# Moving the weights and the staging buffers of a matmul with batch normalisation to multiples of 512 bytes in each partition

## The chip, the cores and the metric

The kernel runs on one core of one Trainium2 chip. The metric is the time of one execution on the device, in microseconds (us); several executions are timed and their median is given. The span that a profile quotes is some 2 us shorter than the timed value, for it runs from the first to the last recorded instruction.

## The reference

The product of x and the weights is normalised per column over all 8192 rows.

```python
batch, m, k, n = 16, 512, 1024, 768          # x: (16, 512, 1024), weight: (1024, 768), float32
y = np.matmul(x, weight)
mean = np.mean(y, axis=(0, 1), keepdims=True)
var = np.var(y, axis=(0, 1), keepdims=True)
y_norm = (y - mean) / np.sqrt(var + eps)
return (gamma * y_norm + beta).astype(np.float32)
```

## The kernel before

The 768 columns are six tiles of 128, and the columns stand on the partitions, so the statistics of a column are sums along one partition. x comes in as bf16 (the DMA casts) through four **staging** buffers of 6144 bytes per partition. VectorE turns it, two bf16 at a time as one float32, into xT, in which even and odd elements of the contraction therefore alternate. TensorE multiplies w (stationary, 128 columns a time) with every second element of xT. When a tile's statistics are complete, y is scaled, transposed back by TensorE, copied as float32 into the *same* staging buffers and stored. The first three column tiles are stored together, in pieces of 384 float32 (1536 B) per row; the last three one at a time, in pieces of 128 float32 (512 B).

```python
    singles = ctx.enter_context(tc.tile_pool(name="singles", bufs=1))
    stage = ctx.enter_context(tc.tile_pool(name="stage", bufs=STAGE))      # STAGE = 4
    xtpool = ctx.enter_context(tc.tile_pool(name="xtpool", bufs=C - EARLY))
    ypool = ctx.enter_context(tc.tile_pool(name="ypool", bufs=...))
    # ... cut
    ident = singles.tile([P, P], bf16)
    eps_sb = singles.tile([P, 1], f32)
    idle_sb = singles.tile([P, CH], bf16)              # operand of the warm-up matmuls
    w_sb = singles.tile([P, JW, 2, N], bf16)
    stats = singles.tile([P, NT, C, 6], f32)
    # ... cut: nine small tiles

    def load_x(q):
        x_bf = stage.tile([P, QT, KQ], bf16, tag="st")
        # ... cut: four DMAs from GpSimd, 32 partitions each

    def mm(nt, c):
        # ... cut
                seq(nc.tensor.matmul(
                    y_ps, w_sb[:, jw, e, nt * P:(nt + 1) * P], xT[c][:, jw, :, e],
                    start=(jw == 0 and e == 0), stop=(jw == JW - 1 and e == 1),
                ))

    def out_copy(key, part, parts, eng):
        # ... cut
            o_sb = stage.tile([P, parts] + list(src.shape[1:]), f32, tag="st")
        # ... cut: ScalarE or VectorE copies the transposed tile from PSUM into o_sb
    def store(key, nts, m0, tiles):
        # ... cut: one DMA of the sync engine from o_sb to the output
```

Tiles are laid out in each partition in the order in which pools and tiles are made. So w came to stand at byte 17824, which is 416 past a multiple of 512, and the staging buffers at 32736, 38880, 45024 and 51168, all 480 past one.

## Time and profile before

| | before |
|---|---|
| time, median of 4 | 230.71 us (230.02 to 231.17) |
| span of the profile | 228.4 us |
| TensorE busy | 207.4 us, 91% |
| last piece of w lands, long run of matmuls starts | 19.56, 19.70 us |
| last matmul of the chain starts | 205.83 us |
| from there to the end of the span | 22.57 us |

The chain that ended last is read in order of time: each line is a start, a length and what held the end up then. Its lines and the DMA rates are shown in the prediction. One line more of the chain of before is of use below, the first transpose back, after the long unbroken run of whole-width matmuls:

```profile
128.65 0.43 PE o_ps L211 x6
```

So the middle has two parts: matmuls alone, 19.70 to 128.65 us, and matmuls mixed with transposes, 128.65 to 205.83 us.

### The profile page before, as it was taken

To read this page: it belongs to the slowest core of one execution; us is meant where nothing else is said; L and a number is where in the kernel's file an instruction comes from. 1 tells how busy PE (TensorE), PEld (TensorE's weight loads), DVE (VectorE), ACT (ScalarE), POOL (GpSimd) and SP (SyncE) were. 2 spreads that over 40 slices of the span, in tenths; PEclk is the share of its full clock that TensorE was granted. 3 is DMA by queue.
4 is the path that set the end of the run, shared out by engine and by line. 5 is a ranking of instruction groups with operands and counts; after the bars stand their busy time and mean duration, and the time that the engine had idled before them with its cause. 6 is when DMAs were issued, how large, how long until landed. Compare 5 with 4: busy or idle time off the path is not lost.

```text
span 228.4 us, 3323 instructions
## 1 busy us (share of the span) xinstructions
PE 207.4 (91%) x1238; PEld 106.0 (46%) x1238; DVE 142.1 (62%) x252; ACT 100.7 (44%) x155; POOL 88.5 (39%) x160
## 2 busy tenths in 40 slices
PE   7767999999999999999999999999999999994720
PEld 2432685444444444444444565655555545553610
DVE  0223769677675777677845968686754476537940
ACT  2001424134233233332633599987696736674310
POOL 8887787678687786878500000000000000003000
PEclk9999999999999999999999999999999999999555
DMA  5999999999999999999000079999989933887996
GB/s 58 180 191 175 191 170 185 173 170 167 161 186 179 167 184 186 163 188 158 1 0 0 4 264 366 362 366 366 337 257 281 258 92 86 225 243 196 270 282 176
DMA packets 69345, 43.75 MB, mean 192 GB/s; under 512 B 3280, under 2 KB 68816, under 8 KB 69328
## 3 DMA queue, kind: packets, MB, share of 16 engines
q0 software_dynamic: 35904, 18.37, 61.3%
q1 hardware_dynamic: 33424, 25.17, 35.5%
q8 instruction: 9, 0.15, 0.2%
q14 instruction: 8, 0.07, 0.1%
HBM read 36.71 MB, written 25.17 MB: 271 GB/s over the span
## 4 chain that ended last, share of the span: by engine, by line
PE 82%; DMA 7%; POOL 3%; DVE 3%; issue 1%; POOLq 0%; ACT 0%; DVEq 0%
PE y_ps L156 67%; PE o_ps L211 8%; PE y_ps L126 7%; DMA w_sb<-in_weight_dram 3%; DMA x_bf<-in_x_dram 2%; DMA out_dram<-o_sb 2%; DVE o_sb L223 2%; POOL w_sb L110 2%; POOL x_bf L138 1%; POOL y_sb L196 0%; POOLq L370 0%; DVE stats L164 0%; DVE y_sb L196 0%; DVE mv L184 0%; ACT std L185 0%
## 5 line engine op out<-in xcount | busy, mean ns | idle before, releaser
L156 PE MATMUL y_ps<-xT_sb,w_sb 128*128 128x512 bf16 x672 | 166.7, 387 | 0.0
L156 PEld LDWEIGHTS <-w_sb 128*128 128x128 bf16 x672 | 64.4, 96 | 85.3
L169 ACT CAST y_sb<-y_ps 128x512 bf16<-128x512 f32 x96 | 56.5, 588 | 93.5 <-DVE stats L164 93.2
L164 DVE BATCH_NORM_STATS2 stats<-y_ps 128x6 f32<-128x512 f32 x96 | 63.5, 681 | 38.4 <-PE y_ps L156 31.6
L138 POOL DMA_DIRECT2D x_bf<-in_x_dram x128 | 73.5, 578 | 23.6 <-issue 9.2
L211 PE MATMUL o_ps<-ident,y_sb 128*128 128x128 bf16 x384 | 62.9, 230 | 5.5 <-DVE y_sb L196 5.1
L149 DVE STREAM_TRANSPOSE xT_sb<-x_bf 128x1024 f32<-128x1024 f32 (+1 forms) x34 | 39.9, 1178 | 34.0 <-DMA x_bf<-in_x_dram 32.9
L221 ACT CAST o_sb<-o_ps 128x768 f32<-128x768 bf16 (+2 forms) x53 | 45.4, 870 | 22.6 <-ACT y_sb L169 10.3
L196 POOL TENSOR_SCALAR y_sb<-y_sb,scale,shift 128x512 bf16<-128x512 bf16 x2 | 1.8, 920 | 96.8 <-DVE shift L191 96.8
L211 PEld LDWEIGHTS <-y_sb 128*128 128x128 bf16 x384 | 33.8, 103 | 9.4 <-DVE y_sb L196 6.2
L196 DVE TENSOR_SCALAR y_sb<-y_sb,scale,shift 128x512 bf16<-128x512 bf16 x94 | 33.5, 412 | 0.0
L126 PE MATMUL y_ps<-xT_sb,w_sb 128*128 128x256 bf16 (+1 forms) x156 | 22.2, 301 | 4.9 <-DMA w_sb<-in_weight_dram 2.9
L126 PEld LDWEIGHTS <-w_sb 128*128 128x128 bf16 x156 | 14.8, 96 | 12.4 <-issue 6.0
L116 PE MATMUL idle_ps<-idle_sb 128*128 128x512 bf16 x26 | 7.9, 475 | 1.2 <-DVE idle_sb L82 1.2
L110 POOL DMA_DIRECT2D w_sb<-in_weight_dram x12 | 6.1, 520 | 0.5 <-issue 0.2
L223 DVE CAST o_sb<-o_ps 128x1024 f32<-128x1024 bf16 x4 | 4.9, 1225 | 2.1 <-DMA out_dram<-o_sb 1.1
L116 PEld LDWEIGHTS <-idle_sb 128*128 128x128 bf16 x26 | 3.0, 117 | 5.6 <-issue 2.8
L103 POOL DMA_DIRECT2D gamma_sb<-in_gamma_dram x6 | 3.3, 552 | 0.3 <-issue 0.2
L104 POOL DMA_DIRECT2D beta_sb<-in_beta_dram x6 | 3.3, 547 | 0.3
L174 DVE BATCH_NORM_AGGREGATE mv<-stats 128x2 f32<-128x96 f32 x5 | 2.6, 559 | 0.0
L176 DVE RECIPROCAL scale<-std 128x1 f32<-128x1 f32 (+1 forms) x3 | 0.5, 168 | 2.5 <-ACT std L175 2.5
L95 ACT ACT_TABLE_LOAD x1 | 1.3, 1283 | 0.7 <-PEq L356 0.7
(19 smaller groups left out, 5.4 us busy)
## 6 DMA issues: line engine op xcount, KB each, us to landing
x_bf<-in_x_dram POOLq DMA_DIRECT2D x128, 128.0 KB, 5.3
out_dram<-o_sb SPq DMA_DIRECT2D x16, 768.0 KB, 4.6
out_dram<-o_sb SPq DMA_DIRECT2D x23, 512.0 KB, 4.1
w_sb<-in_weight_dram POOLq DMA_DIRECT2D x8, 96.0 KB, 4.6
w_sb<-in_weight_dram POOLq DMA_DIRECT2D x4, 192.0 KB, 6.0
out_dram<-o_sb SPq DMA_DIRECT2D x2, 256.0 KB, 2.6
gamma_sb<-in_gamma_dram POOLq DMA_DIRECT2D x6, 0.5 KB, 2.5
beta_sb<-in_beta_dram POOLq DMA_DIRECT2D x6, 0.5 KB, 2.3
```

What stands on the lines that cost most here:

```text
L110: seq(nc.gpsimd.dma_start(dst[32 * i:32 * i + 32, jw:jw1], rows[i, :, jw:jw1]))
L116: seq(nc.tensor.matmul(idle_ps, idle_sb[:, 0:P], idle_sb, start=True, stop=True))
L126: seq(nc.tensor.matmul(py[nt, c][:, q0 * QR:q1 * QR], w_sb[:, jw, e, nt * P:(nt + 1) * P], xT[c][:, jw, q0 * QR:q1 * QR, e], start=(jw == ...
L138: seq(nc.gpsimd.dma_start(x_bf[32 * i:32 * i + 32], rows[:, :, KQ * i:KQ * (i + 1)]))
L149: seq(nc.vector.transpose(dst[:, half, :, jw0:jw1], src[:, :, jw0:jw1]))
L156: seq(nc.tensor.matmul(y_ps, w_sb[:, jw, e, nt * P:(nt + 1) * P], xT[c][:, jw, :, e], start=(jw == 0 and e == 0), stop=(jw == JW - 1 and e ...
L164: seq(nc.vector.bn_stats(stats[:, nt, c, :], py[nt, c]))
L169: seq(nc.scalar.copy(y_sb, py.pop((nt, c))))
L196: seq((nc.vector if eng == "dve" else nc.gpsimd).tensor_scalar(y[nt, c], y[nt, c], scale[:, nt:nt + 1], shift[:, nt:nt + 1], op0=ALU.mult, ...
L211: seq(nc.tensor.transpose(dst, src, ident))
L221: seq(nc.scalar.copy(ost[key][:, part], src))
L223: seq(nc.vector.tensor_copy(ost[key][:, part], src))
```

## The change

The intent is to have w and the staging buffers, which the DMA engines write and read, start at multiples of 512 bytes. A pool is opened first with tiles that fill 512 bytes together with the constants ahead of it; w follows, then staging; the rest comes behind. (Comments in the diffs of this document are added for the reader.)

```diff
+    first = ctx.enter_context(tc.tile_pool(name="first", bufs=1))
+    gamma_sb = first.tile([P, NT], f32)
+    beta_sb = first.tile([P, NT], f32)
+    scale = first.tile([P, NT], f32)
+    shift = first.tile([P, NT], f32)
+    ident = first.tile([P, P], bf16)
+    stage = ctx.enter_context(tc.tile_pool(name="stage", bufs=STAGE))
+    w_sb = first.tile([P, JW, 2, N], bf16)
     singles = ctx.enter_context(tc.tile_pool(name="singles", bufs=1))
-    stage = ctx.enter_context(tc.tile_pool(name="stage", bufs=STAGE))
 ... the six tiles are no longer made in singles; cut
```

w now stands at 16896 and staging at 29184, both multiples of 512. xT (480 past) and y (480 past) stay where they were, and no instruction is added, removed or moved on any engine. Small tiles move too, among them ident, from 128 to 256 past a multiple of 512.

More of the change, by code (lines that the diff above doesn't have):

```diff
@@ L76, in seq @@
         return bi
-    ident = singles.tile([P, P], bf16)
     eps_sb = singles.tile([P, 1], f32)
@@ L82 @@
     seq(nc.vector.memset(idle_sb, 0.0))
-    w_sb = singles.tile([P, JW, 2, N], bf16)
     stats = singles.tile([P, NT, C, 6], f32)
     mv = singles.tile([P, NT, 2], f32)
-    gamma_sb = singles.tile([P, NT], f32)
-    beta_sb = singles.tile([P, NT], f32)
     std = singles.tile([P, NT], f32)
-    scale = singles.tile([P, NT], f32)
     tmp = singles.tile([P, NT], f32)
-    shift = singles.tile([P, NT], f32)
     rstd = singles.tile([P, 1], f32)
```

## The prediction

> **What bounds the kernel now.** I read the page's engine shares first, then the chain that ended last, then the same chain in order of time, then the DMA rates of single stretches. The page opens with the busy shares and closes its fourth part with the chain by engine:
>
> ```profile
> PE 207.4 (91%) x1238; PEld 106.0 (46%) x1238; DVE 142.1 (62%) x252; ACT 100.7 (44%) x155; POOL 88.5 (39%) x160
> ...
> PE 82%; DMA 7%; POOL 3%; DVE 3%; issue 1%; POOLq 0%; ACT 0%; DVEq 0%
> PE y_ps L156 67%; PE o_ps L211 8%; PE y_ps L126 7%; DMA w_sb<-in_weight_dram 3%; DMA x_bf<-in_x_dram 2%; DMA out_dram<-o_sb 2%; DVE o_sb L223 2%; POOL w_sb L110 2%; POOL x_bf L138 1%; POOL y_sb L196 0%; POOLq L370 0%; DVE stats L164 0%; DVE y_sb L196 0%; DVE mv L184 0%; ACT std L185 0%
> ```
>
> TensorE holds 82% of the chain, DMA only 7%. The chain in order of time says where (columns: start in us, length in us, what):
>
> ```profile
> 3.22 5.02 DMA x_bf<-in_x_dram
> ...
> 13.16 6.40 DMA w_sb<-in_weight_dram
> 19.70 16.48 PE y_ps L126 x120
> 36.17 92.48 PE y_ps L156 x408
> ...
> 205.83 0.24 PE y_ps L156
> 206.09 0.71 DVE stats L164
> ...
> 213.72 1.23 DVE o_sb L223
> 214.98 4.32 DMA out_dram<-o_sb
> 219.41 1.23 DVE o_sb L223
> ```
>
> So there are three stages. **Head**, 0 to 19.7 us: loads; the last piece of w lands at 13.16 + 6.40 = 19.56. **Middle**, 19.7 to 206.1: TensorE, link after link, no DMA among them. **Tail**, 206.1 to 228.4: statistics, then normalise, transpose, copy and store the last column tile; a store appears in the chain because a copy waits for its staging buffer. After the last copy (to 220.64) the sync engine's list of waits has one for a landing store, of 4.9 us:
>
> ```profile
> SPq L370 <- DMA out_dram<-o_sb: 4.9, 1, 4.9
> ```
>
> which puts the end of the data near 220.7 + 4.9 = 225.6; some 2.8 us of closing work follow. The tail's DMA rates are in these two stretches (columns as in the table of stretches: length, each engine's busy time and count, granted clock, DMA share, GB/s):
>
> ```profile
> 212.00:220.00 8.00, 4.81 (x40) 4.02 (x40) 6.48 (x14) 2.93 (x3) 0.00 (x0) 0.50 1.00 272
> 220.00:226.00 6.00, 0.00 (x0) 0.00 (x0) 0.64 (x1) 0.00 (x0) 0.00 (x0) 0.50 1.04 286
> ```
>
> The DMA share is 1.00: the tail's end is set by the store rate, 272 to 286 GB/s (290 in the fine slices of the same stretch).
>
> **What the Trainium skill says.** (1) "DMA: Bandwidth & Descriptors", section "How a descriptor splits into AXI transactions": a read must start on a 256-byte boundary; a descriptor that starts off one fetches from the boundary below, and the unused bytes cost 32-byte beats. (2) The same page, "Where 436 GB/s comes from": 16 ports, 32 B per beat, 850 MHz, so 1.18 ns a beat. I work out from both an estimate of what the trace should show, below; it agrees within 5%. (3) "SBUF — State Buffer", section "Operand start alignment", says that engines and DMAs need only element alignment and that this is "about legality, not speed"; no figure for compute engines off a boundary. The trace of before alone cannot show an aligned case.
>
> **The change part by part.** It moves no instruction: set side by side, the two built programs have the same instructions in the same order on all five engines. Only addresses differ. From the tile sizes in order of allocation (each rounded to 32 bytes, the first at 16512): before, w stands at 17824 (416 past a multiple of 512) and the four staging buffers at 32736 plus multiples of 6144 (480 past one). After: w at 16896 and staging at 29184, both multiples of 512. xT (57312) and y (155616) do not move. Staging serves x on its way in and the output on its way out.
>
> *Middle stage: nothing.* The chain gives 92.48/408 = 226.7 ns a matmul. Its moving operand is xT, which does not move. Could w's place matter? The transposes too load new weights for every instruction, from y at 480 past, and the chain shows 11 of them in 0.61 us, 55 ns each. A 128-column weight load from an odd place is thus hidden already. Change: 0 us.
>
> *Stores, read from staging.* A row piece of a one-column-tile store is 128 float32 = 512 B, starting at 480, which is 224 past a 256 boundary. By (1): one 256 B fetch of which 32 B count, one of 256, a rest of 224: 8+8+7 = 23 beats, against 16 when aligned. A piece of the three-tile store is 1536 B: 8+40+7 = 55 beats against 48. At 1.18 ns: 27.1 and 64.7 ns, on 16 engines 303 and 380 GB/s. Measured, in 40 fine slices of 206 to 228 us:
>
> ```profile
> GB/s 290 290 291 58 289 292 283 84 30 209 296 290 158 270 290 264 286 292 248 305 289 262 293 276 275 291 285 261 294 289 268 303 293 285 286 295 174 0 0 15
> ```
>
> and, for the three-tile stores, of 135 to 165 us:
>
> ```profile
> GB/s 356 367 348 379 344 369 369 356 367 381 336 399 354 332 373 375 344 373 373 352 383 369 352 379 360 363 371 365 354 391 360 352 368 360 260 369 375 254 352 373
> ```
>
> 290 GB/s is 28.3 ns a piece (512 x 16 / 290), about 370 is 66.4 ns. Both are the count of beats plus 1.2 to 1.7 ns, so aligned pieces should take 18.8 + 1.5 = 20.3 ns (404 GB/s) at best. The same two points also fit a straight line with 9.7 ns of fixed cost per packet and no alignment in it. The loads decide between them in part: they read 1024 B, aligned, and write 512 B, at a plateau of 193 GB/s written, 42.4 ns a packet, against 37.6 for 32 beats: about 4.8 ns of overhead, not 9.7. With 4.8 an aligned 512 B piece takes 23.6 ns, 347 GB/s. My range is 347 to 404, centre 370.
>
> *The tail with that.* The last column tile is two stores of 256 KB and seven of 512 KB. 512 KB takes 1.81 us at 290 and 1.42 at 370. I ran the queue by hand: a store starts 1 us after its copy ends (copies of the blocks end at 212.2, 212.9, 214.95, 215.6, 217.6, 218.5, 220.6) or after the store before it. Before: from 213.3 seven stores back to back end at 226.0 (the profile: 225.6); the third ends at 218.7, and the wait of the last copy for that store's buffer ends at 219.3 in the chain, so the model is about right. At 370 they end at 223.2: 7 x 0.39 = 2.7 us less; at 347 it is 2.1. At 404 the last copy becomes the limit. It waited 1.15 us for a buffer, but the 8 transposes that feed it only end near 219.03, so it can come just 0.36 us earlier: 3.2 us at most. Tail: **2.1 to 3.2 us, centre 2.5**, if alignment is what slows them.
>
> *The three-tile and middle stores* get faster too, but TensorE holds that stretch: 0 us.
>
> *Head.* x and w are written, not read, at the odd places. Loads plateau at 193 GB/s written, which is 386 read, and the 1024 B read (32 beats) is longer than even 23 beats of writing. So the read side should set the rate: 0 to 0.5 us, centre **0.2**. Were writing the limit, the 14 us of saturated loads before w lands (5.7 to 19.6) would shrink by perhaps 10%, 1.4 us.
>
> **Sum:** 230.92 - 2.5 - 0.2 = 228.2 if the mechanism holds.
>
> **Rivals.** (a) *Fixed cost per packet, or the memory's side of a 512 B write at a 3072 B pitch, sets 290 GB/s.* For: two points fit it equally, and every store is misaligned now, so nothing contradicts it directly. Against: the loads' smaller overhead. It gives 230.5 to 230.9. I give it 30%. (b) *Writes into odd places are what holds loads back.* Then the head gains 1 to 1.5 us on top, and 226.9 or so results; 12%. (c) *The store rate rises but the tail's copies take the bound.* VectorE is busy 6.48 of 8.00 us in 212 to 220; it keeps the gain under 3.2 us and is in my range. (d) *Faster loads crowd something in the middle,* such as GpSimd's port or the staging turn-around: TensorE never waits for x after 19.7, so nothing; slower by over 2% would need a cause I do not see.
>
> **How range and chances follow.** 58% on about 228.2, 30% on about 230.6, 12% on about 226.9; the middle of this mixture is 228.6. The range 226.8 to 230.8 holds all but the outermost of them. Faster by over 2% means under 226.3: it needs rival (b) and the best tail together, 8%. Slower by over 2%: 2%.
>
> **What would show it right or wrong.** Right: 512 B stores at 340 to 400 GB/s in the fine slices of the tail, three-tile stores at 390 or more, the last wait for a landing store down from 4.9 to about 3 us, DMA share below 1 at the end, the time from the last matmul to the end about 2.5 us shorter, matmuls still at 227 ns, w landing within 0.5 us of 19.56. Wrong: the stores still at 290 (rival a), w landing before 18.5 (rival b), or a matmul interval off 227 ns, which would mean that w's place matters to TensorE after all.

## The result, and the profile after

The changed kernel took 227.0 us (median of 4, 226.84 to 227.31), against 230.71 us: a ratio of 0.9843, with a 95% interval of 0.9815 to 0.9872. A ratio is the mean time of one kernel's runs over that of the other's of the same rounds, so it is not quite the ratio of the medians. The prediction was 228.6, within 226.8 to 230.8: right, though the gain, 3.7 us, is more than the 2.3 of its centre.

The chain of the changed kernel in order of time (start, length, what), at the places that answer to those shown of before:

```profile
13.25 6.34 DMA w_sb<-in_weight_dram
19.72 16.44 PE y_ps L129 x120
36.16 91.80 PE y_ps L159 x408
127.96 0.46 PE o_ps L214 x6
...
205.15 0.24 PE y_ps L159
...
215.51 1.23 DVE o_sb L226
216.73 0.33 DVE y_sb L199
217.11 1.05 PE o_ps L214 x8
218.18 1.22 DVE o_sb L226
```

Subtract the marks of one chain from those of the other. w lands at 13.25 + 6.34 = 19.59 us, before 19.56: **the head gave nothing.** From 19.72 to the first transpose it is 108.24 us, before 108.95: **0.71 us less**, and the line of 408 matmuls shows where: 91.80/408 = 225.0 ns from one to the next, before 226.7. From there to the last matmul it is 77.19 us, before 77.18: nothing. From the last matmul to the end of the span it is 225.1 - 205.15 = 19.95 us, before 22.57: **2.62 us less.** The sum is 3.3 us, the whole difference of the spans.

In the tail the DMA wait has left the chain: the last copy now follows the transposes, 218.18 - 215.51 = 2.67 us after the copy before it, where 219.41 - 216.40 = 3.01 us lay before. The two copies of before in its timeline, with the idle time ahead of each and what ended it in brackets:

```profile
216.40 1.23 DVE L223 CAST o_sb<-o_ps 128x1024 f32<-128x1024 bf16 x1 [0.16 <-PE o_ps L211]
219.41 1.23 DVE L223 CAST o_sb<-o_ps 128x1024 f32<-128x1024 bf16 x1 [1.15 <-DMA out_dram<-o_sb]
```

The rest of the gain comes after that copy. The sync engine's wait for the last store, and the two closing stretches of the tail (columns as in the prediction's table of stretches; the last number is GB/s):

```profile
SPq L373 <- DMA out_dram<-o_sb: 3.5, 1, 3.5
```

```profile
212.00:220.00 8.00, 4.51 (x39) 3.72 (x37) 6.23 (x11) 2.02 (x2) 0.00 (x0) 0.50 1.10 333
220.00:225.00 5.00, 0.00 (x0) 0.00 (x0) 0.00 (x0) 0.00 (x0) 0.00 (x0) 0.50 0.67 203
```

The wait went from 4.9 to 3.5 us; the rate in 212 to 220 us rose from 272 to 333 GB/s. The same in 40 fine slices, for 203 to 225.1 us (512 B pieces) and then for 132 to 162 us (1536 B pieces):

```profile
GB/s 331 350 257 0 316 351 282 0 296 346 307 45 0 195 344 349 109 350 346 346 348 348 346 346 349 344 347 349 346 351 343 346 351 343 348 336 12 0 15 0
```

```profile
GB/s 401 403 221 332 397 395 403 410 395 397 401 309 401 384 365 381 262 307 395 395 406 408 397 395 403 315 399 381 373 397 293 279 395 381 159 381 399 143 397 399
```

The plateaus are 346 and about 399 GB/s where they were 290 and about 370. On 16 engines that is 23.7 ns a 512 B piece (512 x 16 / 346), before 28.3, and 61.6 ns a 1536 B piece, before 66.4: 4.6 and 4.8 ns less, whatever the length of the piece. The second gain is worth nothing here: TensorE holds that stretch.

### The profile page after: what moved, and what is told of

Read it like the earlier page. It is cut to its first block, busy times and chain, and to the rows that moved or that the text cites. A ratio compares the mean times of both kernels' runs of the same rounds, so it can differ in the third digit from the quotient of the medians.

```text
span 225.1 us, 3323 instructions
## 1 busy us (share of the span) xinstructions
PE 206.2 (92%) x1238; PEld 105.3 (47%) x1238; DVE 142.1 (63%) x252; ACT 100.7 (45%) x155; POOL 88.4 (39%) x160
## 4 chain that ended last, share of the span: by engine, by line
PE 84%; DMA 5%; DVE 4%; POOL 3%; issue 1%; POOLq 0%; ACT 0%
PE y_ps L159 67%; PE o_ps L214 9%; PE y_ps L129 7%; DMA w_sb<-in_weight_dram 3%; DMA x_bf<-in_x_dram 2%; DVE o_sb L226 2%; POOL w_sb L113 2%; POOL x_bf L141 1%; DVE y_sb L199 1%; POOL y_sb L199 0%; POOLq L373 0%; DVE stats L167 0%; DVE mv L187 0%; ACT std L188 0%; DVE rstd L192 0%
## 5 line engine op out<-in xcount | busy, mean ns | idle before, releaser
L214 PEld LDWEIGHTS <-y_sb 128*128 128x128 bf16 x384 | 33.3, 101 | 9.7 <-DVE y_sb L199 6.5
```

Source lines behind the costliest of these rows:

```text
L214: seq(nc.tensor.transpose(dst, src, ident))
```

## The experiments

The theory after the result: stores read from a staging place off a boundary cost a fixed time per piece (2.6 us in the tail), w's place costs TensorE 1.7 ns a matmul (0.7 us), and x's place costs nothing. The rivals: all of it is the stores and the matmul interval is chance of a chip; the loads gain as well; the cost grows with the bytes fetched in vain. Twelve kernels were run, four at a time on one chip. This table puts all profiles side by side; it is worked out from the starts of the matmul records, which lie some 0.15 us before the marks of the chain. The numbers under w, output and xT are bytes past a multiple of 512. "To transpose" is the start of the first transpose back, "mixed" from there to the last matmul, "tail" from the last matmul to the end of the span, all in us; "ns" is the interval of back-to-back whole-width matmuls; GB/s the plateau of 512 B stores.

| run | w | output | xT | to transpose | ns | mixed | tail | GB/s | ratio to before |
|---|---|---|---|---|---|---|---|---|---|
| before | 416 | 480 | 480 | 128.49 | 226.7 | 77.18 | 22.71 | 290 | |
| after | 0 | 0 | 480 | 127.80 | 225.0 | 77.19 | 20.12 | 346 | 0.9843 |
| e1, before again | 416 | 480 | 480 | 128.47 | 226.7 | 77.17 | 22.75 | 290 | 1.0003 |
| e2, w alone | 0 | 480 | 480 | 127.09 | 225.0 | 77.19 | 22.74 | 290 | 0.9937 |
| e3, staging alone | 416 | 0 | 480 | 127.28 | 226.7 | 77.19 | 20.34 | 346 | 0.9892 |
| e4, output alone | 416 | 0 | 480 | 128.27 | 226.7 | 77.18 | 20.14 | 346 | 0.9889 |
| e5, xT and y too | 0 | 0 | 0 | 127.74 | 225.8 | 77.22 | 20.33 | 346 | 0.9888 |
| e6, at 32 | 32 | 32 | 480 | 128.73 | 226.7 | 77.19 | 22.74 | 290 | 1.0014 |
| e7, at 128 | 128 | 128 | 480 | 131.06 | 226.7 | 77.19 | 22.70 | 290 | 1.0025 |
| e8, at 256 | 256 | 256 | 480 | 127.79 | 225.0 | 77.18 | 20.13 | 346 | 0.9845 |
| e9, contiguous xT reads | 0 | 0 | 480 | 124.72 | 215.8 | 74.93 | 20.34 | 346 | 0.9608 |
| e10, w alone again | 0 | 480 | 480 | 127.20 | 225.0 | 77.18 | 22.74 | 290 | 0.9987 |
| e11, xT at 128 | 0 | 0 | 128 | 128.96 | 225.0 | 77.17 | 20.34 | 346 | 0.9872 |
| e12, after again | 0 | 0 | 480 | 128.87 | 225.0 | 77.18 | 20.34 | 346 | 0.9897 |

Three columns fall into groups with nothing between them: the interval, the tail and the store rate. The fourth, to the transpose, scatters by 4 us (e9 apart) without regard to the layout; see e12.

### e1: the kernel before again

No edit.

> A control: the kernel before, unchanged, timed against itself. Every theory expects a ratio of 1.000 within 0.003. It also settles one open number: back-to-back 512-column matmuls stood 226.7 ns apart in the profile before and 225.0 ns in the one after. If that is a difference between chips or executions, this profile will show some other value, the same as in the other runs of this set; if w's place makes it, this one shows 226.7 and w alone shows 225.0.

Measured: 230.46 us against 229.97, ratio 1.0003 (0.9969 to 1.0037); matmuls 226.7 ns apart. The interval is not a matter of the chip. It also shows what a ratio of six runs can tell: 0.35% either way, about 0.8 us, too coarse for parts of 0.7 us; those are read from the stages.

### e2: w alone

```diff
     w_sb = first.tile([P, JW, 2, N], bf16)        # at a multiple of 512, as in the change
+    pad_b = first.tile([P, 120], f32)             # staging back to 480 past one
     warm = singles.tile([P, 1], f32)
+    pad32 = singles.tile([P, 8], f32)             # xT stays 480 past one
```

> Only w moves to a multiple of 512; staging stays at 480 past one. Theory (stores read from an odd place cost time, nothing else matters): no change, 230.7 us, ratio 1.000 within 0.003, 512-byte stores still at 290 GB/s. Rival (w's place makes each matmul 1.7 ns slower): about 672 x 1.7 ns = 1.1 us less at most, ratio near 0.996, matmuls 225.0 ns apart here and in no run with w at 416.

Measured: 228.8 us, ratio 0.9937 (0.9913 to 0.9961). The stores stayed at 290 GB/s, but the matmuls stand 225.0 ns apart. Two links of its chain, and below them two of e7, where w is off again (49 matmuls; one record in 50 is missing from these traces, so a link's period holds 50):

```profile
58.24 11.19 PE y_ps L161 x49
69.49 11.19 PE y_ps L161 x49
```

```profile
61.70 11.27 PE y_ps L162 x49
73.03 11.27 PE y_ps L162 x49
```

(69.49 - 58.24)/50 = 225.0 ns; (73.03 - 61.70)/50 = 226.6 ns. The theory that only stores matter is wrong, and the rival is right: w's place is worth 0.7 us in the run of matmuls. The ratio says 1.4 us; the rest is the start of the middle, 19.01 us here, which e10 tests.

### e3: staging alone

```diff
+    pad_a = first.tile([P, 104], f32)             # w at 416 past a multiple of 512
     w_sb = first.tile([P, JW, 2, N], bf16)
+    pad_b = first.tile([P, 24], f32)              # staging at a multiple
```

> Only staging moves to multiples of 512; w stays at 416 past one. Theory: nearly all of the gain, 227.0 to 228.0 us, ratio 0.984 to 0.988, 512-byte stores at 346 GB/s, three-tile stores near 397 GB/s. Rival (w's place): only the store part, 2.6 us of tail, ratio 0.988 to 0.990, matmuls at 226.7 ns apart.

Measured: 227.85 us, ratio 0.9892 (0.9862 to 0.9923); tail 20.34 us, matmuls at 226.7 ns. Neither expectation's interval alone is excluded by the ratio; the stages decide: the tail has its whole gain, the interval none.

### e4: only the output within staging

The kernel before, with buffers of 6656 bytes (13 x 512), in which x starts at the front (480 past) and the output 32 bytes further (a multiple of 512).

```diff
-        x_bf = stage.tile([P, QT, KQ], bf16, tag="st")
+        x_raw = stage.tile([P, QT * KQ + 1280], bf16, tag="st")
+        x_bf = x_raw[:, 0:0 + QT * KQ].rearrange("p (t k) -> p t k", k=KQ)
-            o_sb = stage.tile([P, parts] + list(src.shape[1:]), f32, tag="st")
+            s_, a_, n_ = src.shape[1:]
+            o_raw = stage.tile([P, parts * s_ * a_ * n_ + 8], f32, tag="st")
+            o_sb = o_raw[:, 8:].rearrange("p (q s a n) -> p q s a n", q=parts, s=s_, a=a_)
```

> Only the output pieces inside the staging buffers move to multiples of 512 (32 bytes further in a longer buffer); x is still written at 480 past one and w stays at 416. Theory: the same as staging alone within 0.003, since the loads gain nothing from their place (w landed at 19.56 us before and 19.59 after). Rival (the place that x is written to also matters): slower than staging alone by over 0.5 us.

Measured: 227.63 us, ratio 0.9889 (0.9864 to 0.9914), the same as staging alone, and the same plateaus. So where x is written is worth nothing that shows (each ratio is good to some 0.3%, 0.7 us): what counts in the staging buffers is the place that stores read from.

### e5: xT and y at multiples of 512 as well

```diff
     warm = singles.tile([P, 1], f32)
+    pad32 = singles.tile([P, 8], f32)             # xT to 57344, y to 155648
```

> The changed kernel with xT and y, too, at multiples of 512 (32 bytes further). Back-to-back matmuls stand 226.7 ns apart with w at 416 and 225.0 with w at 0; the warm-up matmuls, whose moving operand is contiguous, stand 216 ns apart. Theory A (a place off the boundary costs each operand that TensorE reads, and xT at 480 carries a part of the remaining 9 ns): matmuls well under 225, towards 216 ns, so up to 6 us less in all. Theory B (only the weight load's place counts; the 9 ns belong to the moving operand's step of two elements): still 225.0 ns, ratio to before as in the changed kernel, 0.984. Theory C (it is the place of w and xT relative to each other): some other value, perhaps 226.7 again.

Measured: 227.86 us, ratio 0.9888 (0.9867 to 0.9909). The interval is 225.8 ns:

```profile
58.63 11.23 PE y_ps L160 x49
69.93 11.23 PE y_ps L160 x49
```

(69.93 - 58.63)/50 = 226.0, and 225.8 over all. Not less than 225.0, as theory A had it, but 0.8 ns more, as theory C allowed. Lining up everything is thus not better than the change. xT and y moved together here, so the 0.8 ns may belong to either. Transposes, which load y as weights, stayed at 55 ns with y at 0 as with y at 480.

### e6, e7, e8: w and the output at 32, 128 and 256

x stays at a multiple of 512 and xT at 480 past one; buffers of 6656 bytes as in e4. For e6 (in e7 and e8 8 becomes 32 and 64, and 120 becomes 96 and 64):

```diff
+    pad_a = first.tile([P, 8], f32)
     w_sb = first.tile([P, JW, 2, N], bf16)
+    pad_b = first.tile([P, 120], f32)
... the lines of load_x as in e4; cut
-            o_sb = stage.tile([P, parts] + list(src.shape[1:]), f32, tag="st")
+            s_, a_, n_ = src.shape[1:]
+            o_raw = stage.tile([P, parts * s_ * a_ * n_ + 8], f32, tag="st")
+            o_sb = o_raw[:, 8:].rearrange("p (q s a n) -> p q s a n", q=parts, s=s_, a=a_)
```

> w at 32 and the output pieces at 32 past a multiple of 512, x still written at a multiple. Stores of 512 B ran at 290 GB/s (28.3 ns a piece) from 480 and at 346 (23.7 ns) from 0. By the count of beats, scaled to that 4.6 ns for 7 beats, 1 beat more costs 0.7 ns: 24.4 ns, 336 GB/s. By the rival that one more transaction costs a fixed 4.6 ns: 290 GB/s. For w: if any place off a multiple of 256 costs TensorE 1.7 ns, matmuls 226.7 ns apart; if only crossing a longer line does, 225.0.

> w and the output pieces at 128 past a multiple of 512. By scaled beats, 4 more: 26.3 ns a piece, 311 GB/s. By the fixed cost of one more transaction: 290 GB/s. If only being off a multiple of 64 or 128 counts: 346 GB/s. For w: 226.7 ns between matmuls if 256 is the unit, 225.0 if it is 128 or less.

> w and the output pieces at 256 past a multiple of 512. If the unit is 256 bytes, as both the count of beats and the rival of one more transaction have it: stores as fast as from 0, 346 GB/s, and a time like the changed kernel's, ratio 0.984. If the unit is 512: 290 GB/s. For w: 225.0 ns if the unit is 256 or less, 226.7 if it is 512.

Measured: at 32, 230.89 us, ratio 1.0014 (0.9994 to 1.0034); at 128, 230.61 us, 1.0025 (0.9989 to 1.0061); at 256, 227.04 us, 0.9845 (0.9824 to 0.9866). The fine slices of 203 to 226 us, for 32, 128 and 256:

```profile
GB/s 242 115 289 291 217 139 290 290 192 165 290 292 165 43 43 291 284 264 259 288 268 286 291 258 292 280 278 287 251 307 289 260 299 289 273 299 288 282 297 288
```

```profile
GB/s 279 79 292 294 252 104 290 290 228 131 289 290 202 158 289 289 176 43 136 290 287 199 235 289 267 289 292 258 298 275 279 286 255 304 290 261 296 290 272 293
```

```profile
GB/s 341 345 212 38 347 345 181 70 346 349 146 43 49 347 344 172 291 348 344 349 347 344 349 348 345 348 346 347 351 343 348 346 346 348 195 0 0 14 0 0
```

290, 290 and 346. Being 32 bytes off costs as much as 128 or 480, and 256 costs nothing. **The unit is 256 bytes, and the cost of missing it is the same at all three places tried**, 4.6 ns a piece; it doesn't grow with the bytes fetched in vain, which would have given 336 and 311 GB/s. The records of single 512 B packets do lengthen with the place (mean 27.0 ns at 0, 256 and 32, 28.3 at 128, 29.6 at 480), but they overlap (27.0 ns recorded where each of the 16 engines ends one every 23.7), so it is the rate that counts. The matmul interval has the same unit: 226.7, 226.7 and 225.0 ns. A slice of w that one load reads is 128 bf16 = 256 bytes per partition, so w on a multiple of 256 keeps each slice within one 256-byte unit, and any other place splits it over two.

### e9: contiguous reads of xT (a wrong result)

```diff
-                    y_ps, w_sb[:, jw, e, nt * P:(nt + 1) * P], xT[c][:, jw, :, e],
+                    y_ps, w_sb[:, jw, e, nt * P:(nt + 1) * P],
+                    xT[c].rearrange("p jw m e -> p jw (m e)")[:, jw, e * CH:(e + 1) * CH],
```

> Wrong result on purpose: the changed kernel, whose whole-width matmuls in the middle read 512 neighbouring elements of xT in place of every second one; the bytes are wrong, the amount of work is the same. It measures what the remaining 9 ns of the 225.0 ns between matmuls are. If they are the moving operand's step of two elements: 216 ns, as in the warm-up matmuls, about 408 x 9 = 3.7 us less in the middle and about 223.5 us in all. If they come with loading new weights: still 225 ns and 227 us.

Measured: 221.24 us, ratio 0.9608 (0.9583 to 0.9633); wrong result, as meant.

```profile
69.90 10.74 PE y_ps L159 x49
80.69 10.74 PE y_ps L159 x49
```

(80.69 - 69.90)/50 = 215.8 ns. The step of two elements in the moving operand is what the other 9 ns are. It is more than expected in all, because the matmuls among the transposes profit too: the mixed part takes 74.93 in place of 77.18 us.

### e10: w alone again

The program of e2.

> Only w moved, the same program as the earlier run of w alone, which came out at a ratio of 0.9937 (1.4 us) while its stages showed 0.7 us in the middle and 0.7 us of an earlier start of the middle. If w's place also makes the loads of the head quicker: again a ratio near 0.994 and a start near 19.0 us. If the earlier start was chance, as the 18.5 to 20.7 us of the other profiles suggest: a ratio near 0.997 (0.7 of 230.6 us), and the start anywhere in that span.

Measured: 230.0 us, ratio 0.9987 (0.9957 to 1.0016); the start of the long run is at 19.12 us, the interval 225.0 ns, the tail 22.74 us. The start is early again, yet the ratio is not; the two ratios average 0.996, 0.9 us, in line with the 0.7 us of the interval. The two early starts (19.01, 19.12) lie within the 18.5 to 20.7 us of the others (e3, with w off, has the earliest, 18.49), so no gain in the head is shown, and one of a few tenths is not excluded.

### e11: xT at 128

```diff
     warm = singles.tile([P, 1], f32)
+    pad = singles.tile([P, 40], f32)              # xT and y at 128 past a multiple of 512
```

> The changed kernel with xT and y at 128 past a multiple of 512, in place of 480. With xT at 0 and w at 0 matmuls stood 225.8 ns apart, with xT at 480 and w at 0 225.0. If xT's place matters by itself and 0 is a worse place than others: 225.0 or less. If 480 was a lucky place: 225.8 or more. In all: within 0.5 us of the changed kernel, stores unchanged at 346 GB/s.

Measured: 227.22 us, ratio 0.9872 (0.9847 to 0.9896); matmuls 225.0 ns apart. So 480 was not a lucky place; 0, for xT or for y, which moved with it, is a slightly worse one (e5). Why is open: worth 0.4 us, it was not followed further.

### e12: the changed kernel again

No edit.

> The changed kernel unchanged, timed on the same chip as the three others: ratio 0.984 within 0.003, matmuls 225.0 ns apart, stores at 346 GB/s, 20.1 us from the last matmul to the end; the start of the middle is where chance may put it (18.5 to 20.7 us).

Measured: 227.52 us, ratio 0.9897 (0.9863 to 0.9930), a smaller gain than first measured (0.9843, 0.9815 to 0.9872; the two intervals overlap narrowly); matmul interval, stores and tail are the same. Its profile shows what scatters: in the head TensorE was granted half its clock for a while (the number before the last two):

```profile
10.00:15.00 5.00, 1.52 (x12) 1.17 (x13) 1.10 (x3) 0.00 (x0) 3.96 (x8) 1.00 1.20 156
15.00:20.00 5.00, 4.65 (x20) 2.51 (x21) 0.67 (x2) 0.00 (x0) 4.36 (x10) 0.66 1.12 203
```

0.66 over 5 us is one window of 3.4 us at 0.5. In the first profile of this kernel both stretches were at 1.00. Here TensorE idled 1.8 us after the warm-up, worked 1.5, idled 2.5 more for the second x block, and the clock fell: the first transpose came at 128.87 in place of 127.80 us. Five of the fourteen profiles have such a window of 3.4 or 6.8 us in the first 36 us: e1, e7, e9, e11 and e12. TensorE worked in all of them. In e1 (11.0 to 14.4 us) that cost nothing, for it waited for w afterwards in any case and the first transpose came at 128.47; e11 and e12 came to it some 1.1 us later than the first profile of the changed kernel.

What sets the clock down can be read from the 14 heads. The clock's records come in steps of 3.41 us; laid out in these steps, the five in which TensorE, at full clock, idled for 1.98 to 2.55 us by its records were followed by half clock, and none in which it idled for up to 1.91 us was. So the same waits cost nothing or a microsecond, according to how they fall in the steps. In the tail, among transposes, this limit doesn't hold (1.59 and 1.73 us of idling were enough in e8 and after).

This noise of the head is the likeliest reason why the ratios of one program differ, 0.9843 and 0.9897; not every timed execution has a trace, so it is not shown for all. By the two measurements the change gains 2.4 to 3.6 us.

## Why the prediction was right or wrong

- **"The middle stage: nothing" was wrong, by 0.7 us.** The step that failed is that w's place could not matter because "a 128-column weight load from an odd place is thus hidden already". It argued from transposes, whose moving operand is contiguous. The run of whole-width matmuls reads its moving operand with a step of two, and there w's place costs 1.7 ns each (e2, e6, e7 against after and e8), 408 x 1.7 = 0.7 us. The argument holds where it was observed: transposes stay at 55 ns, the mixed part at 77.2 us, and the warm-up matmuls, contiguous too, stood at 216 ns with their weights 416 or 32 past a multiple of 512. The starts of the matmul records show how narrow the loss is. In the mixed part a matmul starts 55 ns after the transpose before it with w at 416 as with w at 0, and a transpose 226.1 to 226.6 ns after the matmul before it at every place of w and y (e9 apart); only the 31 or 32 pairs of matmuls with no transpose between them show the loss, 226.5 to 226.6 against 225.0 to 225.1 ns (e5 apart). The 256-column matmuls of the head, stepped as well, stand 113.3 ns apart before and after. So the loss is shown where a stepped 512-column matmul directly follows another with w misplaced, and nowhere else here; a split slice beside a stepped operand is not enough, and what else it takes is open. Stepped and contiguous reads in the long run beside the same misplaced w were not run.
- **The stores: right in kind, with the cost per piece mis-sized and then well bracketed.** Rival (a), 30%, that alignment has no part in it, is refuted by e3 to e8. The count of beats, 7 x 1.18 = 8.2 ns a piece, is too: 4.6 to 4.8 ns was measured, and the same for 1 beat as for 7 (e6). Its fit to both rates of before was a coincidence of two points with two unknowns. (The line without alignment has 9.2 ns of fixed cost through the two points; 9.7 is the mean where 1.18 ns a beat is kept.) The other end of the bracket, from the overhead of the loads, was right: 347 GB/s expected, 346 measured. One more transaction per piece, since a piece off a multiple of 256 crosses one boundary more, would give a fixed cost, but that is not shown, and the aligned pieces speak against a price per transaction: 1536 B have four more units of 256 B than 512 B and take 61.6 - 23.7 = 37.9 ns longer, which the prediction's 1.18 ns a beat (32 beats, 37.8 ns) uses up. The runs show only that the cost is fixed and that its unit is 256; what makes it is open.
- **The tail: 2.6 us, centre 2.5, in part by luck.** Over all profiles it is 22.70 to 22.75 us where stores start off a multiple of 256, and 20.12 to 20.34 where they start on one: 2.4 to 2.6 us less. The centre was worked out at 370 GB/s; at the 346 that was measured the hand-run queue gives only 2.1. A rate that was too high and a queue that gained too little made up for each other. The last copy came 0.34 us earlier for want of a buffer wait (0.36 predicted). The end of the last store was put at 225.6 by adding the wait to the end of the copy; the last issue itself took long there, 0.98 us (220.66 to 221.64) where the first of these takes 0.37. The trace shows the issues merged:

```profile
202.73 18.91 SPq L227 DMA_DIRECT2D out_dram<-o_sb  x12
```

  The issues end at 202.73 + 18.91 = 221.64, so the store landed near 226.5, and after near 223.3 (the issues end at 219.81, and 3.5 us of wait follow). That is 3.2 us between the landings, of which 0.68 are the earlier end of the matmuls. Before is thus where the queue was off: it had 226.0 for 226.5, while for after 226.0 - 2.1 - 0.68 = 223.2 is close to the 223.3 found. Two signs came out otherwise than forecast: the last wait fell to 3.5 us, not to about 3, and the DMA share in 212 to 220 us rose to 1.10, where it was to fall below 1. The stores still set the end.
- **Three-tile stores: right.** 399 GB/s ("390 or more"), and no time gained, for the mixed part did not move.
- **The head: 0.2 us expected, none seen.** Loads stay at the plateau of 190 to 197 GB/s in both kernels, and e4 equals e3. Rival (b) is refuted: the 12% laid on it had a wrong reason, and that the result lies near its 226.9 us is owed to w (0.7 us) and to chance instead.
- **Sum.** 2.6 (tail) + 0.7 (w) = 3.3 us, as the spans differ; the forecast's mechanism had 2.7, and the weight on rival (a) drew the centre down to 2.3.

## What to carry to other kernels

Look at the start of every SBUF tile that a DMA stores from in short pieces, and of a stationary operand whose slices are 256 bytes; here a multiple of 256 bytes was best for both, and it cost only the order in which tiles are made. It paid where stores set the end, in the last 20 us (2.4 to 2.6 us), and not where they ran under TensorE; for w it was 0.7 us. When two explanations fit two numbers equally, look for the place where they part (here 32 bytes off) before trusting either. The largest thing found is untried as a working kernel: a moving operand without the step of two took 221.2 us (e9), and would need xT split into even and odd halves at less than that cost.

## What the Trainium skill lacked or had wrong

- "DMA: Bandwidth & Descriptors", "How a descriptor splits into AXI transactions": the 256-byte boundary is right, but the count of beats does not give the cost. Stores of 512 B from 32, 128 and 480 past a multiple of 512 all ran at 290 GB/s, from 0 and 256 at 346; 4.6 ns a piece, and 4.8 for pieces of 1536 B (480 against 0). The page words the rule on the start for reads, and the runs agree: writing x at 480 past showed no cost, 190 to 197 GB/s either way.
- "SBUF — State Buffer", "Operand start alignment", is about legality alone. For speed: w off a multiple of 256 makes back-to-back matmuls with a stepped moving operand 226.7 in place of 225.0 ns. xT, with y moved alike, at 0, 128 and 480 gave 225.8, 225.0 and 225.0 ns; no page explains that.
- "TensorE: Matmul & The Clock Gate", "Wait — 56ns, not 53.3ns?", gives N / 2.4 GHz plus about 2.5 ns, 215.8 for 512 columns. Contiguous reads agree, 216 ns. The page has nothing for a bf16 moving operand with a step of two elements, 225 ns here; "SBUF — State Buffer", under "Door 1: The DMA port swizzle (why `[64,N]` ≈ `[32,N]`)", says that bf16 can be read with a step of up to 8 elements for free, and in these matmuls a step of two cost 9 ns.
- "TensorE: Matmul & The Clock Gate", "What's actually happening", has the clock at half after an idle window of about 3.4 us. The traces agree on the length (3.4 and 6.8 us), but the window need not be idle throughout: in the heads 1.98 to 2.55 us of idling within one were enough and up to 1.91 us were not (e12).
